# Rotary features gathered into two and a half projection tiles, and attention loads that gather the heads

## The chip, the cores and the metric

The kernel runs on one core of a Trainium2 chip. The metric is the device time of one execution in microseconds (us). The engines are named as in the profile: PE does matmuls (PEld is its weight load), DVE, ACT and POOL work on vectors, SP issues the DMAs. This kernel issues every DMA from SP.

## The reference, cut to what matters

One decoder layer runs over 1024 prompt tokens and 8 rows of 8 sampled tokens, 1088 tokens in all. One input projection feeds two groups: sliding-window attention with 16 query heads on 4 key/value heads (head dimension 64), and a Mamba-2 state-space group (SSD). Their outputs go through one output projection, and a SwiGLU feed-forward follows. Only the first 16 of a head's 64 features are rotated:

```python
q, k, v, z, xbc, dt_raw = jnp.split(h @ w_in, SPLIT_IDX, axis=-1)
q = rope_partial(q.reshape(b, L, ATT_HEADS, HEAD_DIM), pos)
k = rope_partial(k.reshape(b, L, ATT_KV_HEADS, HEAD_DIM), pos)

def rope_partial(x, pos):                 # ROT_DIM = HEAD_DIM // 4 = 16, half = 8
    xr = x[..., :ROT_DIM].astype(F32)
    x1, x2 = xr[..., :half], xr[..., half:]
    rot = jnp.concatenate([x1 * cos - x2 * sin, x2 * cos + x1 * sin], axis=-1)
    return jnp.concatenate([rot.astype(x.dtype), x[..., ROT_DIM:]], axis=-1)
```

Three results depend on the rotated keys beside the layer's output: the last 128 keys of the prompt are an output (`new_k_prompt`), and the sampled tokens' keys join the cached ones.

## The kernel before

**Tiling.** Activations lie feature-major: 128 features on the partitions, tokens along the row, in three chunks of 384, 384 and 320 tokens (`CH`). A weight tile is 1024 x 128: `load_w` (L118) brings it in two halves of 256 KB, ACT casts each to its high part (L123), POOL subtracts for the low part (L124). `gemm` (L133) multiplies in three passes (lines 140 to 142). One unit of the input projection (`in_unit`, L281) is one weight tile by one chunk: 24 matmuls into one of two PSUM buffers ("mm", the profile's `ip`), then an evacuation, which frees the buffer.

**Two evacuations.** `spill_evac` (L483) is one DVE multiply of PSUM by the row scale `Rx` into a staging tile (`stg`, L486), and a DMA to scratch in DRAM (L487). `rope_evac` (L678) is for rotated tiles: ACT copies PSUM to `ra` (L681), DVE shuffles partitions into `rb` (L683), POOL multiplies `rb` by the sine table (L684), DVE multiplies `ra` by the cosine table (L685) and adds both (L686), and a DMA goes to scratch (L687). The tables carry the row scale, and hold one and zero for features that do not rotate. Each head's 64 features stand together, so every q and k tile holds some rotated features: of the twelve tiles of `kvq` (L690), ten go through `rope_evac` (30 units) and two, the values, through `spill_evac` (6 units). `z_proj` follows with eight more spilled tiles.

**Order.** PE's order is written by hand: `weave(mixer, filler)` (L157) lets the mixer run, and the filler fill the time that the mixer grants. In the stage of this change the mixer is the SSD over its eight prompt chunks and the sampled tokens (`ssd`, with `ssd_a`, L515, and `ssd_b`, L573), and the filler is `kvq`, then `z_proj`, then the first output projection (L698 to L700). In the attention stage the filler goes on with `z_proj` and the output projection. The order on DVE, ACT, POOL and SP is set by a tile scheduler from the order of the code and from priorities; evacuations and weight loads are marked urgent. Once set, each engine runs strictly in its order.

**SSD names.** `d_0...` and `d_1...` are the two groups. `YI` are PSUM products of a chunk, evacuated into `y` on DVE (L584). For the sampled tokens, `xh` (ACT, L590) and `xw` (DVE, L591) are the split operand of the state products `H` (L635, L636); POOL scales the old state (`d_0h`, L638) and DVE adds `H` (L640).

**Attention.** `blk_a` (L725) handles one block of 128 tokens and one pair of key heads (16 in all): it loads q by one DMA (L730), k by two (L733) and v by one (L735), PE transposes v (`vt`, L737), ACT casts k (`KW`, L742), and ACT and POOL split q (`A`, L749 and L750). Its load buffers are double. `att_sample` (L837) loads the same things once for the sampled tokens, by six DMAs (L849 to L851). The last 128 keys go to their output by two DRAM-to-DRAM copies (`o_kp`, L811).

Of the kernel before, what the change touches and what calls it, by code (L numbers as in the profile page):

```python
# [23 lines left out]
HD = 64  # L24
NFF = 22
# [9 lines left out]
def hybrid_layer(ctx, tc, A):  # L35
# [26 lines left out]
    # split operands of a chunk in half tiles of four feature tiles each, in numbered slots  # L62
# [37 lines left out]
    class Extra:  # L100
        # weight slots cut out of a larger tile
# [31 lines left out]
    def gemm(out, ws, xs, step=3, only=None):  # L133
        # three passes of split operands; yields the time on the tensor engine
# [18 lines left out]
    def weave(mixer, filler):  # L153
        # the filler yields its time on the tensor engine, or None while its operands are not there;
        # the mixer yields how long the filler may hold the tensor engine before it goes on
        credit = 0.0
        for gap in mixer:  # L157
            credit += gap
            while credit > 0:
                try:  # L160
                    cost = next(filler)
                except StopIteration:
                    break
                if cost is None:
                    break
                credit -= cost
# [4 lines left out]
    def rsqrt_cols(st, nb, inv, name):  # L171
        # 1/sqrt(st * inv + eps), one token per partition: bit-level first guess, Newton to float32
# [14 lines left out]
    def rms(groups, n, inv, name, gap, keep=None):  # L187
        # groups of tiles; the sum over a group's tiles and partitions is the sum of squares of each token
# [32 lines left out]

    def finish(gen):
# [6 lines left out]
    # scratch in DRAM  # L229
    q_scr = [dr.tile([P, 4, TOK], F32, name="q_scr%d" % p) for p in range(2)]  # L230
    k_scr = [dr.tile([P, TOK], F32, name="k_scr%d" % p) for p in range(2)]
# [104 lines left out]
    with pool("conv") as cvp:  # L336
# [38 lines left out]
        with pool("norm") as tp:  # L375
# [15 lines left out]
            # the tensor engine's clock comes up while the first operands are on their way  # L391
# [11 lines left out]
            def dt_mm(c, k):  # L403
                # four feature tiles at a time, in four column groups of the array
# [19 lines left out]
            # the first chunk by feature tile, as they come in; its evacuation waits for the row scale  # L424
# [82 lines left out]
    with pool("ssd") as sd, pool("rope") as rp:  # L507
# [5 lines left out]
        def ssd_a(c, gi):  # L513
            # token-major x scaled by dt and by the tail decay; masked C.B; decay weights
# [154 lines left out]
        shuf = list(range(8, 16)) + list(range(8)) + list(range(16, 32))  # L669
# [8 lines left out]
        def rope_evac(dst):  # L678
            def f(c, c0, n, o):
                a = rp.tile([P, n], F32, tag="ra", bufs=2, name="ra")  # L680
                s.copy(a, o)  # L681
                b = rp.tile([P, n], F32, tag="rb", bufs=2, name="rb")
                v.stream_shuffle(b, a, shuf)  # L683
                g.tensor_mul(b, b, sinT[:, c0:c0 + n])  # L684
                v.tensor_mul(a, a, cosT[:, c0:c0 + n])  # L685
                v.tensor_add(a, a, b)  # L686
                dma(dst[:, c0:c0 + n], a)  # L687
            return f

        def kvq():  # L690
            for p in range(2):
                yield from in_proj(2 * p, rope_evac(k_scr[p]))
                yield from in_proj(2 * p + 1, spill_evac(v_scr[p]))
            for gi in range(4):
                for p in range(2):
                    yield from in_proj(4 + 4 * p + gi, rope_evac(q_scr[p][:, gi, :]))
            done.add("q")
# [27 lines left out]
    def blk_a(ap, n, p, KW, vts):  # L725
# [4 lines left out]
        dma(qb, q_scr[p][:, :, b0:b0 + P])  # L730
        kd = ap.tile([P, 2, P], F32, tag="kd", bufs=2, name=nm + "k")
        for hh in range(2):
            dma(kd[HD * hh:HD * hh + HD], k_scr[p][:, b0:b0 + P].rearrange("(e f) t -> f e t", e=2))  # L733
# [76 lines left out]
    for p in range(2):  # L810
        dma(A["o_kp"][p], k_scr[p][:, SEQ - P:SEQ])  # L811
# [24 lines left out]
    # sampled tokens: one batch row at a time, all heads on the rows  # L836
    def att_sample(ap):  # L837
# [9 lines left out]
        with tc.high_priority():  # L847
            for p in range(2):
                dma(qs[p], q_scr[p][:, :, SEQ:])  # L849
                dma(kvn[:, p, 0, :], k_scr[p][:, SEQ:])  # L850
# [77 lines left out]
    def gate(c, at=None):  # L928
        # y * silu(z), its norm, and the split of the result
# [131 lines left out]
    with pool("chain") as kp:  # L1061
        # the first FFN tiles go chunk by chunk
# [23 lines left out]
    with pool("ffn") as fp:  # L1086
        # the cache rows that only move up, in the time when little else is loaded
# [5 lines left out]
        for gi, G in enumerate(FFG):  # L1093
# [51 lines left out]
            else:  # L1145
                # the last feature tiles go chunk by chunk, with the last norm and the residual behind them
# [17 lines left out]
                for c, (c0, n) in enumerate(CH):  # L1164
# [13 lines left out]
                    # the second feature tile's operands come in behind the first one's products  # L1178
# [21 lines left out]
def _consts():  # L1200
# [16 lines left out]
    cos = np.ones((P, TOK), f)  # L1217
    sin = np.zeros((P, TOK), f)
    for e in range(2):
        o = e * HD  # L1220
        cos[o:o + 8] = co
        cos[o + 8:o + 16] = co
        sin[o:o + 8] = -si
        sin[o + 8:o + 16] = si
# [12 lines left out]
def _layout(x):  # L1237
# [10 lines left out]
    q = w[:, 0:1024].reshape(DM, 2, 2, 4, HD).transpose(0, 1, 3, 2, 4).reshape(DM, 1024)  # L1248
    k, v_, z = w[:, 1024:1280], w[:, 1280:1536], w[:, 1536:2560]
    xs, bcm, dt = w[:, 2560:3584], w[:, 3584:4096], w[:, 4096:4112]  # L1250
    d["w_in"] = blk(np.concatenate([k[:, :P], v_[:, :P], k[:, P:], v_[:, P:], q, bcm, xs, z], 1))
# [58 lines left out]
```

## Time and profile before

| what | value |
|---|---|
| median of 3 runs | 1768.01 us (1766.32 to 1768.69) |
| span of the profiled execution | 1755.4 us |
| PE busy in it | 1650.0 us, 94% |
| DVE, ACT, POOL busy | 931.4, 629.0, 659.3 us |

The profile is of one execution; its span runs from its first to its last recorded instruction. The 12.6 us between span and median lie outside what the trace records. The stage of this change is the stretch from 190 to 455 us (keys, values and queries beside the SSD), and the attention stage is 455 to 735 us.

### The profile page before, as it was taken

Reading aid. Unit: us, or ns where it says so; the run is one execution under the profiler, and the core shown is the slowest. Engines: PE = TensorE matmul, PEld = TensorE weight load, DVE = VectorE, ACT = ScalarE, POOL = GpSimd, SP = SyncE. Lnnn points to the kernel's source line nnn. Section 1 sums busy time; section 2 is a strip of 40 time slices with the busy share of each in tenths; the row PEclk is TensorE's granted clock in tenths of the full one; section 3 lists DMA queues with packets and bytes.
Section 4 is the critical chain, followed back from the end, with each engine's and each line's share of the span. In section 5 each row is a group of like instructions: output and inputs, shape, how many; then the busy total and the mean of one; then the engine's idle time right before and its main releaser. Section 6 shows DMA issues by size and latency. Waiting matters only on the chain. (4 is left out here: it accounts for less than half of the span.)

```text
span 1755.4 us, 26644 instructions
## 1 busy us (share of the span) xinstructions
PE 1650.0 (94%) x9959; PEld 1553.4 (88%) x9959; DVE 931.4 (53%) x1977; ACT 629.0 (36%) x1416; POOL 659.3 (38%) x537
## 2 busy tenths in 40 slices
PE   9899998888888998999988999999999999999995
PEld 6899987766776787898987999999999999999995
DVE  7796778886588898455877401221312212121347
ACT  5242344441376676554543332112121121211221
POOL 5262366666743333323655322222222221221432
PEclk9899999998999999999999999999999999999997
DMA  5022564444652351543554111111111111110233
GB/s 184 30 85 101 166 177 136 134 125 157 208 153 84 93 156 59 167 148 94 180 179 141 47 49 32 49 52 32 55 41 47 44 38 49 41 55 22 82 102 102
DMA packets 144945, 171.12 MB, mean 97 GB/s; under 512 B 16624, under 2 KB 105200, under 8 KB 144784
## 3 DMA queue, kind: packets, MB, share of 16 engines
q1 hardware_dynamic: 144816, 169.43, 31.6%
q8 instruction: 78, 1.28, 0.3%
q14 instruction: 51, 0.42, 0.1%
HBM read 135.33 MB, written 36.28 MB: 98 GB/s over the span
## 5 line engine op out<-in xcount | busy, mean ns | idle before, releaser
L1027 DVE TENSOR_TENSOR sg<-sg,ou 128x384 f32<-128x384 f32 (+1 forms) x66 | 35.0, 531 | 393.4 <-PE ou L142 392.7
L1138 DVE TENSOR_TENSOR YP<-YP,od 128x384 f32<-128x384 f32 (+1 forms) x168 | 89.0, 531 | 126.9 <-PE od L142 126.7
L124 POOL TENSOR_TENSOR wg_1l<-wg_1r,wg_1h 128x512 fp32r<-128x512 f32 x20 | 25.9, 1295 | 211.5 <-ACT wg_1h L123 211.5
L1028 ACT CAST ffh<-sg 128x384 fp32r<-128x384 f32 (+1 forms) x66 | 32.6, 495 | 188.9 <-DVE sg L1027 188.5
L124 POOL TENSOR_TENSOR wi_1l<-wi_1r,wi_1h 128x512 fp32r<-128x512 f32 x40 | 56.7, 1418 | 63.7 <-ACT wi_1h L123 60.2
L1023 ACT ACTIVATE sg<-og 128x384 f32<-128x384 f32 (+1 forms) x66 | 31.0, 471 | 131.9 <-PE og L142 125.2
L124 POOL TENSOR_TENSOR wi_0l<-wi_0r,wi_0h 128x512 fp32r<-128x512 f32 x40 | 58.3, 1458 | 30.6 <-ACT wi_0h L123 26.2
L1029 DVE TENSOR_TENSOR ffl<-sg,ffh 128x384 fp32r<-128x384 f32 (+1 forms) x66 | 42.8, 649 | 33.9 <-ACT ffh L1028 33.8
L140 PE MATMUL ip<-x1h,wi_0h 128*128 128x384 f32 x128 | 48.0, 375 | 11.8 <-ACT ra L681 5.2
L124 POOL TENSOR_TENSOR wos_1l<-wos_1r,wos_1h 128x512 fp32r<-128x512 f32 x24 | 33.1, 1377 | 65.3 <-ACT wos_1h L123 58.3
L124 POOL TENSOR_TENSOR woa_1l<-woa_1r,woa_1h 128x512 fp32r<-128x512 f32 x24 | 35.0, 1456 | 49.6 <-ACT woa_1h L123 38.4
L363 DVE SCALAR_TENSOR_TENSOR cacc<-cbuf,vec,cacc 128x1112 f32<-128x1112 f32 x36 | 52.3, 1455 | 0.7
L140 PE MATMUL ip<-x0h,wi_0h 128*128 128x384 f32 x128 | 47.4, 371 | 3.5 <-DVE cbuf L350 3.5
L124 POOL TENSOR_TENSOR wd_1l<-wd_1r,wd_1h 128x384 fp32r<-128x384 f32 (+1 forms) x7 | 6.8, 974 | 105.2 <-ACT wd_1h L123 105.2
L140 PE MATMUL ip<-x0h,wi_1h 128*128 128x384 f32 x128 | 45.6, 356 | 0.0
L142 PE MATMUL ip<-x0h,wi_0l 128*128 128x384 f32 x128 | 44.0, 344 | 1.5 <-POOL wi_0l L124 1.5
L140 PE MATMUL ip<-x1h,wi_1h 128*128 128x384 f32 x128 | 45.1, 353 | 0.0
L124 POOL TENSOR_TENSOR wg_0l<-wg_0r,wg_0h 128x512 fp32r<-128x512 f32 x21 | 27.4, 1304 | 45.6 <-ACT wg_0h L123 45.6
L142 PE MATMUL ip<-x1h,wi_0l 128*128 128x384 f32 x128 | 44.3, 346 | 0.0
L141 PE MATMUL ip<-x0l,wi_0h 128*128 128x384 f32 x128 | 43.8, 342 | 0.4 <-DVE x0l L261 0.4
L141 PE MATMUL ip<-x1l,wi_0h 128*128 128x384 f32 x128 | 44.2, 345 | 0.0
L684 POOL TENSOR_TENSOR rb<-rb,sinT 128x384 f32<-128x384 f32 (+1 forms) x30 | 36.0, 1198 | 21.2 <-DVE rb L683 17.5
(837 smaller groups left out, 6215.0 us busy)
## 6 DMA issues: line engine op xcount, KB each, us to landing
wi_0r<-in_w_in SPq DMA_DIRECT2D x40, 256.0 KB
wi_1r<-in_w_in SPq DMA_DIRECT2D x40, 256.0 KB
wos_0r<-in_w_os SPq DMA_DIRECT2D x24, 256.0 KB
wos_1r<-in_w_os SPq DMA_DIRECT2D x24, 256.0 KB
woa_0r<-in_w_oa SPq DMA_DIRECT2D x24, 256.0 KB
woa_1r<-in_w_oa SPq DMA_DIRECT2D x24, 256.0 KB
wg_0r<-in_w_g SPq DMA_DIRECT2D x22, 256.0 KB
wg_1r<-in_w_g SPq DMA_DIRECT2D x22, 256.0 KB
```

The costliest lines, as they stand in the source:

```text
L124: (eng or g).tensor_sub(lo, raw, fr(hi))
L140: t.matmul(out, lhsT=wh, rhs=xh, start=k == 0, stop=False)
L141: t.matmul(out, lhsT=wh, rhs=xl, start=False, stop=False)
L142: t.matmul(out, lhsT=wl, rhs=xh, start=False, stop=k == n - 1)
L363: v.scalar_tensor_tensor(acc[:, :L], buf[:, k:k + L], vec[:, cw + k:cw + k + 1], acc[:, :L], ALU.mult, ALU.add)
L684: g.tensor_mul(b, b, sinT[:, c0:c0 + n])
L1023: s.activation(sg, og[:, :n], AF.Silu)
L1027: v.tensor_mul(sg, sg, ou[:, :n])
L1028: s.copy(hi[:, c0:c0 + n], sg)
L1029: v.tensor_sub(lo[:, c0:c0 + n], sg, fr(hi[:, c0:c0 + n]))
L1138: v.tensor_add(YP[m][:, c0:c0 + n], YP[m][:, c0:c0 + n], o[:, :n])
```

## The change

The host permutes the columns of `w_in` for q and k so that the rotated features of all heads stand together. The twelve tiles become: tile 0, 64 rotated key features and 64 key features that do not rotate; tile 1, the other 128 of those; tiles 2 and 3, values; tiles 4 and 5, the rotated query features of either pair of key heads; tiles 6 to 11, all other query features. Tiles 4 and 5 go through `rope_evac` whole, tile 0 in its first 64 partitions, with one DVE multiply for the rest. That makes 9 units with rotation (three of them with the extra multiply) and 27 that are spilled. The scratch tensors `q_scr` and `k_scr` become `qr_scr`, `qn_scr`, `kr_scr` and `kn_scr`, and each load puts the heads together again: per attention block four DMAs for q and four for k instead of one and two, for the sampled tokens 16 instead of four beside the two of v, and four for `o_kp` instead of two.

```diff
+    def load_q(dst, p, t0, n):
+        for e in range(2):
+            for o, w, src in ((0, ROT, qr_scr[p]), (ROT, NRT, qn_scr[p])):
+                dma(dst[HD * e + o:HD * e + o + w],
+                    src[:, t0:t0 + n].rearrange("(g e r) t -> e r g t", g=4, e=2)[e])
+
+    def k_rows(p, t0, n):
+        for o, w, src in ((0, ROT, kr_scr), (ROT, NRT, kn_scr)):
+            yield o, w, src[2 * p * w:2 * p * w + 2 * w, t0:t0 + n].rearrange("(e r) t -> e r t", e=2)
...
-        def rope_evac(dst):
+        def rope_evac(dst, m=P, rest=None):
             def f(c, c0, n, o):
                 a = rp.tile([P, n], F32, tag="ra", bufs=2, name="ra")
-                s.copy(a, o)
+                s.copy(a[:m], o[:m])
                 b = rp.tile([P, n], F32, tag="rb", bufs=2, name="rb")
-                v.stream_shuffle(b, a, shuf)
-                g.tensor_mul(b, b, sinT[:, c0:c0 + n])
-                v.tensor_mul(a, a, cosT[:, c0:c0 + n])
-                v.tensor_add(a, a, b)
-                dma(dst[:, c0:c0 + n], a)
+                v.stream_shuffle(b[:m], a[:m], shuf)
+                g.tensor_mul(b[:m], b[:m], sinT[:m, c0:c0 + n])
+                v.tensor_mul(a[:m], a[:m], cosT[:m, c0:c0 + n])
+                v.tensor_add(a[:m], a[:m], b[:m])
+                dma(dst[:, c0:c0 + n], a[:m])
+                if rest is not None:
+                    x = stage(n, "stg")
+                    v.tensor_mul(x[m:], o[m:], Rx[c][m:])
+                    dma(rest[:, c0:c0 + n], x[m:])
             return f

         def kvq():
+            yield from in_proj(0, rope_evac(kr_scr, HD, kn_scr[0:HD]))
+            yield from in_proj(1, spill_evac(kn_scr[HD:]))
             for p in range(2):
-                yield from in_proj(2 * p, rope_evac(k_scr[p]))
-                yield from in_proj(2 * p + 1, spill_evac(v_scr[p]))
-            for gi in range(4):
-                for p in range(2):
-                    yield from in_proj(4 + 4 * p + gi, rope_evac(q_scr[p][:, gi, :]))
+                yield from in_proj(2 + p, spill_evac(v_scr[p]))
+            for p in range(2):
+                yield from in_proj(4 + p, rope_evac(qr_scr[p]))
+            for i in range(6):
+                yield from in_proj(6 + i, spill_evac(qn_scr[i // 3][P * (i % 3):P * (i % 3) + P]))
...
-        dma(qb, q_scr[p][:, :, b0:b0 + P])
+        load_q(qb, p, b0, P)
...
-            dma(kd[HD * hh:HD * hh + HD], k_scr[p][:, b0:b0 + P].rearrange("(e f) t -> f e t", e=2))
+            for o, w, src in k_rows(p, b0, P):
+                dma(kd[HD * hh + o:HD * hh + o + w], src.rearrange("e r t -> r e t"))
...
-        dma(A["o_kp"][p], k_scr[p][:, SEQ - P:SEQ])
+        for o, w, src in k_rows(p, SEQ - P, P):
+            dma(A["o_kp"][p].rearrange("(e f) t -> e f t", e=2)[:, o:o + w, :], src)
...
-                dma(qs[p], q_scr[p][:, :, SEQ:])
-                dma(kvn[:, p, 0, :], k_scr[p][:, SEQ:])
+                load_q(qs[p], p, SEQ, NS)
+                for o, w, src in k_rows(p, SEQ, NS):
+                    for e in range(2):
+                        dma(kvn[HD * e + o:HD * e + o + w, p, 0, :], src[e])
```

The cosine and sine tables now repeat over all partitions, and the shuffle pattern swaps eights in all 32 lanes. PE's order stays the same, matmul for matmul, but for the names of weights. What moves stands on the other engines.

**DVE, sampled tokens.** DVE's order around the sampled tokens' `d_0xw`, on which PE's state products wait. Before:

```order
L544 TENSOR_TENSOR d_1cb<-d_1bc,cst 64x64
L551 TENSOR_SCALAR d_1W<-d_1ac,ADT 64x64 x4
L584 SCALAR_TENSOR_TENSOR d_0y<-d_0xb,vec,d_0YI 128x64 x4
L683 STREAM_SHUFFLE rb<-ra 128x384
L685 TENSOR_TENSOR ra<-ra,cosT 128x384
L591 TENSOR_TENSOR d_0xw<-d_0xtl,d_0xh 64x512
L686 TENSOR_TENSOR ra<-ra,rb 128x384
```

and now:

```order
L561 TENSOR_TENSOR d_1cb<-d_1bc,cst 64x64
L568 TENSOR_SCALAR d_1W<-d_1ac,ADT 64x64 x4
L601 SCALAR_TENSOR_TENSOR d_0y<-d_0xb,vec,d_0YI 128x64 x2
L503 TENSOR_TENSOR stg<-ip,rs1Rk 128x384
L601 SCALAR_TENSOR_TENSOR d_0y<-d_0xb,vec,d_0YI 128x64 x2
L608 TENSOR_TENSOR d_0xw<-d_0xtl,d_0xh 64x512
```

The three rotary steps around `d_0xw` became one multiply from PSUM, inside the `d_0y` group. On POOL the row `rb<-rb,sinT` between `d_1W` and the weight subtraction `wi_1l` is gone; `wi_1l` and the four scalings of `d_0h` still follow.

**DVE, middle of the stage.** DVE's order at a change of SSD chunk in the stretch that is all queries. Before:

```order
L544 TENSOR_TENSOR d_1cb<-d_1bc,cst 128x128
L683 STREAM_SHUFFLE rb<-ra 128x384
L584 SCALAR_TENSOR_TENSOR d_0y<-d_0xb,vec,d_0YI 128x128
L685 TENSOR_TENSOR ra<-ra,cosT 128x384
L584 SCALAR_TENSOR_TENSOR d_0y<-d_0xb,vec,d_0YI 128x128
L686 TENSOR_TENSOR ra<-ra,rb 128x384
L584 SCALAR_TENSOR_TENSOR d_0y<-d_0xb,vec,d_0YI 128x128 x2
```

and now:

```order
L547 TENSOR_TENSOR d_1xdt<-d_1xT,ADT 128x512
L548 TENSOR_TENSOR d_1xtl<-d_1xT,ADT 128x512
L561 TENSOR_TENSOR d_1cb<-d_1bc,cst 128x128
L503 TENSOR_TENSOR stg<-ip,rs1Rk 128x384
L601 SCALAR_TENSOR_TENSOR d_0y<-d_0xb,vec,d_0YI 128x128 x4
```

The rotary steps that stood between the four `d_0y` rows are gone, and one multiply stands ahead of them.

**SP, start of the attention stage.** SP's order of DMA issues from the first query load to the first value load (`a_0q`, `a_0k` and `a_0vb` are a block's q, k and v; `wi` are halves of a `z` weight tile). Before:

```order
L730 DMA a_0q<-q_scr_78 128x4x128
L487 DMA z_scr<-stg 128x384
L120 DMA wi_0r<-in_w_in 128x512
L733 DMA a_0k<-k_scr_80 64x2x128 x2
L120 DMA wi_1r<-in_w_in 128x512
L735 DMA a_0vb<-v_scr_82 128x128
```

and now, from the fourth row on (ahead of it stand the first `qr_scr` load, a `z_scr` spill and a `wi_0r`):

```order
L228 DMA a_0q<-qn_scr_80 48x4x128
L122 DMA wi_1r<-in_w_in 128x512
L228 DMA a_0q<-qr_scr_78 16x4x128
L228 DMA a_0q<-qn_scr_80 48x4x128
L504 DMA z_scr<-stg 128x384
L122 DMA wi_0r<-in_w_in 128x512
L758 DMA a_0k<-kr_scr 16x2x128
L122 DMA wi_1r<-in_w_in 128x512
L758 DMA a_0k<-kn_scr 48x2x128
L758 DMA a_0k<-kr_scr 16x2x128
L758 DMA a_0k<-kn_scr 48x2x128
L760 DMA a_0vb<-v_scr_84 128x128
```

The value load is now the 15th issue from the first query load, where it was the seventh: eight loads of q and k stand ahead of it instead of three, two spills instead of one, and four weight halves instead of two.

## Rows read from the trace of the kernel before

**Rows 1.** Part 1 of the page: busy time, share of the span, instructions.

```profile
PE 1650.0 (94%) x9959; PEld 1553.4 (88%) x9959; DVE 931.4 (53%) x1977; ACT 629.0 (36%) x1416; POOL 659.3 (38%) x537
```

**Rows 2.** Stretches: bounds; us, PE, PEld, DVE, ACT, POOL busy (x); clock, DMA share, GB/s.

```profile
205.00:265.00 60.00, 59.19 (x416) 53.24 (x415) 47.07 (x99) 31.39 (x78) 35.46 (x24) 1.00 0.70 195
265.00:378.00 113.00, 98.00 (x674) 85.83 (x672) 93.89 (x187) 50.05 (x124) 75.10 (x54) 0.98 0.47 131
378.00:410.00 32.00, 21.89 (x97) 17.00 (x96) 23.39 (x37) 6.80 (x17) 16.88 (x14) 0.73 0.34 114
...
265.00:302.00 37.00, 32.92 (x223) 29.64 (x221) 30.24 (x61) 16.07 (x41) 24.33 (x18) 0.95 0.46 129
302.00:378.00 76.00, 65.09 (x453) 56.20 (x452) 63.64 (x127) 33.97 (x84) 50.77 (x37) 1.00 0.47 132
```

**Rows 3.** Waits of PE, 265 to 378 us: total us, times, longest.

```profile
PE ip L140 <- ACT ra L681: 5.2, 4, 1.8
PE d_0YI L580 <- DVE d_1y L584: 4.4, 4, 2.0
```

**Rows 4.** Waits of PE, 378 to 410 us.

```profile
PE d_0H L636 <- DVE d_0xw L591: 6.9, 1, 6.9
PE d_0YI L580 <- DVE d_1y L584: 1.6, 1, 1.6
```

**Rows 5.** Instructions on tile ra by stretch: length, DVE, ACT busy, clock, DMA.

```profile
205.00:265.00 60.00, 9.42 (x15) 1.83 (x4) 1.00 0.70 195
265.00:378.00 113.00, 42.15 (x57) 6.32 (x14) 0.98 0.47 131
```

**Rows 6.** Tiles ra and stg, 190 to 455 us: ns min/median/max, starts, forms.

```profile
L685 DVE TENSOR_TENSOR ra<-ra,cosT x30: 493/1110/2226, 194.5 to 445.0; 128x384 f32<-128x384 f32 x20, 128x320 f32<-128x320 f32 x10
...
L486 DVE TENSOR_TENSOR stg<-ip,rs0Rk x10: 547/554/558, 206.5 to 507.8; 128x384 f32<-128x384 f32 x10
```

**Rows 7.** Line L591 on DVE; POOL's timeline from 394 us (start, us).

```profile
L591 DVE TENSOR_TENSOR d_0xw<-d_0xtl,d_0xh x1: 6747/6747/6747, 394.5 to 394.5; 64x512 fp32r<-64x512 f32 x1
L591 DVE TENSOR_TENSOR d_1xw<-d_1xtl,d_1xh x1: 676/676/676, 430.4 to 430.4; 64x512 fp32r<-64x512 f32 x1
...
394.03 1.35 POOL L684 TENSOR_TENSOR rb<-rb,sinT 128x384 f32<-128x384 f32 x1
395.35 1.25 POOL L124 TENSOR_TENSOR wi_1l<-wi_1r,wi_1h 128x512 fp32r<-128x512 f32 x1
396.56 4.09 POOL L638 TENSOR_TENSOR d_0h<-d_0h,d_0en 128x512 f32<-128x512 f32 x4
```

**Rows 8.** SP's issues of attention loads: ns min/median/max, starts.

```profile
L730 SPq DMA_DIRECT2D a_0q<-q_scr x8: 549/557/614, 458.3 to 632.8; - x8
...
L733 SPq DMA_DIRECT2D a_1k<-k_scr x16: 574/590/1222, 467.4 to 649.5; - x16
```

**Rows 9.** Timeline of SP and PE as the attention starts.

```profile
458.31 0.61 SPq L730 DMA_DIRECT2D a_0q<-q_scr  x1
462.08 0.44 SPq L735 DMA_DIRECT2D a_0vb<-v_scr  x1
...
465.64 0.30 PE L737 MATMUL a_0vt<-cst,a_0vb 128*128 128x128 f32 x1 [1.38 <-DMA wi_1r<-in_w_in]
472.64 0.33 PE L737 MATMUL a_1vt<-cst,a_1vb 128*128 128x128 f32 x1 [2.25 <-DMA a_1vb<-v_scr]
```

**Rows 10.** Timeline of SP and ACT, a key load and its first use.

```profile
571.51 1.24 SPq L733 DMA_DIRECT2D a_0k<-k_scr  x2
...
598.08 0.41 ACT L742 CAST KW<-a_0k 128x256 fp32r<-128x256 f32 x1
```

**Rows 11.** Timeline of SP, ACT and PE behind the sampled tokens' loads.

```profile
732.88 1.59 SPq L120 DMA_DIRECT2D woa_0r<-in_w_oa  x1
...
740.99 0.62 ACT L123 CAST woa_0h<-woa_0r 128x512 fp32r<-128x512 f32 x1 [5.09 <-DMA woa_0r<-in_w_oa]
...
745.73 0.34 PE L140 MATMUL op<-o0h,woa_0h 128*128 128x384 f32 x1
```

More of the change, by code (lines that the diff above doesn't have):

```diff
@@ L24 @@
 HD = 64
+ROT = 16
+NRT = HD - ROT
 NFF = 22
@@ L227, in finish @@
             return e.value
-    q_scr = [dr.tile([P, 4, TOK], F32, name="q_scr%d" % p) for p in range(2)]
-    k_scr = [dr.tile([P, TOK], F32, name="k_scr%d" % p) for p in range(2)]
+    qr_scr = [dr.tile([P, TOK], F32, name="qr_scr%d" % p) for p in range(2)]
+    qn_scr = [dr.tile([3 * P, TOK], F32, name="qn_scr%d" % p) for p in range(2)]
+    kr_scr = dr.tile([4 * ROT, TOK], F32, name="kr_scr")
+    kn_scr = dr.tile([4 * NRT, TOK], F32, name="kn_scr")
     v_scr = [dr.tile([P, TOK], F32, name="v_scr%d" % p) for p in range(2)]
@@ L666, in ssd @@
             yield from ssd_b(prev)
-        shuf = list(range(8, 16)) + list(range(8)) + list(range(16, 32))
+        shuf = [16 * i + (j + 8) % 16 for i in range(2) for j in range(16)]
         cosT = rp.tile([P, TOK], F32, name="cosT")
@@ L1216, in _consts @@
     co, si = np.cos(ang), np.sin(ang)
[L1217 to L1224, printed above, removed]
+    cos = np.tile(co, (P // 8, 1))
+    sin = np.tile(np.concatenate([-si, si], 0), (P // ROT, 1))
     scanm = np.ones((16, TOK), f)
@@ L1246, in blk, with flat @@
         return m.reshape(kk // P, P, mm // P, P).transpose(2, 1, 0, 3)
-    q = w[:, 0:1024].reshape(DM, 2, 2, 4, HD).transpose(0, 1, 3, 2, 4).reshape(DM, 1024)
-    k, v_, z = w[:, 1024:1280], w[:, 1280:1536], w[:, 1536:2560]
+    q = w[:, 0:1024].reshape(DM, 2, 2, 4, HD).transpose(0, 1, 3, 2, 4)
+    k, v_, z = w[:, 1024:1280].reshape(DM, 4, HD), w[:, 1280:1536], w[:, 1536:2560]
+    def flat(m):
+        return m.reshape(DM, -1)
     xs, bcm, dt = w[:, 2560:3584], w[:, 3584:4096], w[:, 4096:4112]
-    d["w_in"] = blk(np.concatenate([k[:, :P], v_[:, :P], k[:, P:], v_[:, P:], q, bcm, xs, z], 1))
+    d["w_in"] = blk(np.concatenate([flat(k[..., :ROT]), flat(k[..., ROT:]), v_, flat(q[..., :ROT]),
+                                    flat(q[..., ROT:]), bcm, xs, z], 1))
     d["w_dt"] = np.pad(dt.reshape(8, P, 16).transpose(1, 0, 2), ((0, 0), (0, 0), (0, 16)))
```

## The prediction, made before the changed kernel was run

> **What bounds the kernel now.** I read the page's busy times first: PE is busy 94% of the span, no other engine over 53% [rows 1]. PE's matmuls and their order are untouched, so the change can gain only what PE loses in gaps, plus matmul time lost to a low clock. Next I cut the stage into stretches [rows 2]. From 205 to 265 us, with half of the units rotated, PE idles 60.00 - 59.19 = 0.8 us. From 265 to 378 us, where every filler unit is a rotated query tile, it idles 113.00 - 98.00 = 15.0 us. From 378 to 410 us, around the first sampled-token group, it idles 32.00 - 21.89 = 10.1 us, with a mean clock of 0.73. What differs between the first two is rotary work: on tile `ra` alone DVE spends 42.15 us of 113 in the second, 9.42 of 60 in the first [rows 5]; in the second it stands still for 113.00 - 93.89 = 19 us even so [rows 2], so order counts as well as load. PE's own waits say the same: in the middle stretch it waits for the PSUM buffer that ACT's rotary copy frees (5.2 us) and for SSD products that DVE evacuates late (4.4 us for `d_1y`) [rows 3]; in the next, once for 6.9 us for `d_0xw` on DVE, and 1.6 us for `d_1y` [rows 4].
>
> **Middle stretch: forecast -10, bounds 0 to -15.** Of 30 rotated units 9 remain, so 21 lose three DVE operations, an ACT copy and a POOL multiply, and get one DVE multiply (three more serve the mixed tile, so 24 multiplies are added). Where they remain matters: tiles 4 and 5, rotated whole, are the first query tiles, six units that stand where the first six of the 57 / 3 = 19 rotated units of this stretch stood [rows 5]. That is its first third, 265 to 302 us, whose idle time, 37.00 - 32.92 = 4.1 us [rows 2], I leave as it is. In the other 76 us some 13 units lose their rotation. A rotated unit's DVE work is 3 x 42.15 / 57 = 2.2 us [rows 5], the multiply instead 0.55 [rows 6]: 13 x 1.65 = 21 us less, so DVE there falls from 63.64 us [rows 2] to about 43, a busy share of 0.56, below the 0.78 (47.07 of 60) of the stretch that PE crosses almost without idling [rows 2], and the ACT and POOL steps leave the chain that frees PSUM. These 76 us hold 76.00 - 65.09 = 10.9 us of idle time [rows 2], of which I leave 0.8 x 76 / 60 = 1.0: -9.9, taken as -10. Upper end: all 15.0 us, if relief behind the first third reaches into it. Lower end: nothing, if the gaps come from strictly ordered queues, whatever stands in them.
>
> **Sampled tokens: forecast -12, bounds 0 to -18.** `d_0xw` took 6747 ns, its twin `d_1xw` 676 for the same shape [rows 7]. It started at 394.5 and ended at 401.2, while POOL ran six instructions without a gap, 394.03 to 400.65. The first of the six is a rotary multiply, and it is gone. Then POOL goes from `d_1W` to the weight subtraction `wi_1l`, which must wait for ACT's cast of that tile; in the gap `d_0xw` can run. In the order it stands ahead, but DVE now has one more PSUM multiply and half of `d_0y` before it, so that it may still meet the scalings of `d_0h`. I put the gap at some 2 in 3 and take the wait as gone: -6.9 and -1.6 of the `d_1y` wait [rows 4]. The low clock goes with it. A mean of 0.73 between the levels 1.0 and 0.5 (2.4 and 1.2 GHz) means 54% of 32 us, or 17 us, at the low one; if the 8.5 us of those waits lie in it, some 8.5 us of matmuls ran at half speed and would take 4.3 less. Sum -12.8; I take -12 and leave some for a shorter wait. Upper end: all idle time, 10.1, and all the clock's loss with it, 17 x 0.5 = 8.5, makes -18. Lower end: `d_0xw` is held again, 0.
>
> What the row shows is an instruction held through six POOL instructions [rows 7]. The Trainium skill ("SBUF — State Buffer", section "Who interferes with whom") says that a VectorE instruction with two SBUF inputs is blocked by a GpSimd instruction that reads SBUF until that one is done, and that one with at most one SBUF input is not. By the rule alone the hold would end with the instruction in progress, the gap would not be needed, and the -12 would be sure; the sum would be the same, and rival 1 less likely. The trace speaks against a hold of one instruction; it agrees on the second half: the spill multiply, one input from PSUM, never left 547 to 558 ns, where the two-input multiply spread from 493 to 2226 [rows 6].
>
> Gains together: -22.
>
> **Loads at the attention's start: forecast +5, bounds 0 to +10.** Issues of the old loads take 0.56 and 0.59 us [rows 8]; I take 0.6 for each new one, since these two differ by 0.03 us where one moves four times the other's bytes. Before, the first value load was issued 462.08 - 458.31 = 3.8 us after the first query load, and PE's transpose of it started at 465.64, so just 3.6 us later, after a wait [rows 9]. Now it is the 15th issue: five more gathers, one more spill and two more weight halves. 14 x 0.6 = 8.4 us, 4.6 more. One of the halves needs a raw buffer that POOL frees behind its first split of `a_0q`, whose loads come later too: about 1 us. PE waited 1.4 us there already, so no slack hides it: 4.6 to 5.6 us. The second block's transpose waited 2.2 us at 472.64 and gets five more issues, 3 us, inside the same delay. I take +5. Upper end: the two delays add, 5.6 + 3, and some clock. Lower end: PE is late enough with the `z` tiles that stand before the transpose.
>
> **The other loads of the attention: +1, bounds 0 to +5.** Each of the other 14 blocks has five issues more, 2.9 us of SP. In the steady part a key load is issued at 571.51 and first used at 598.08 [rows 10]: 26.6 us ahead, which hides 2.9. Some early blocks have less.
>
> **Sampled tokens' loads: +3.5, bounds 0 to +6.** There are 12 issues more (18 for 6), 12 x 0.6 = 7.2 us, ahead of the weight `woa_0r`. Issued at 732.88, its cast started at 740.99, and PE used it at 745.73 [rows 11]. From the cast's end (0.62 us) and a POOL subtraction of 1.25 (as in [rows 7]) to that use are 745.73 - 740.99 - 0.62 - 1.25 = 2.9 us of slack, and a little more, since the low part is used in the third pass only; I take 3.7. 7.2 - 3.7 = 3.5. Upper end: a shortage of weights goes on over the next tiles; lower end: buffers ahead of it absorb it.
>
> **Key output and other spills: +0.5, bounds 0 to +2.** `o_kp` makes two more issues, nothing waits for them but their place on SP; the mixed tile's second part adds three stores, in a stretch where PE idles 0.8 us. Column order, tables and host work cost nothing on the chip.
>
> Costs together +10, net -12. The profiled span is 1755.4 us; the 12.6 us between it and the median lie outside it and are carried over. 1768.0 - 12 = **1756.0 us**.
>
> **Rivals.** (1) *`d_0xw` is held again.* DVE comes to it late and meets the four scalings of `d_0h`; of the -12 only -1 is left. -10 - 1 + 10 = -1: 1767.0 us. For it: the hold outlasted the one rotary multiply by five instructions [rows 7]. Against it: the gap before `wi_1l`. Chance 0.22. (2) *Slower: the gathers are dear to issue.* The dearest issue of a key load took 1222 ns against a median of 590 [rows 8]. If each gather of 16 or 48 partitions takes that, 32 gathers that nothing hides (8 in each of the first two blocks, 16 for the sampled tokens) cost 32 x 0.64 = 20.5 us more; with the net -12 that is +8.5: 1776.5 us. It makes the kernel slower from 12 / 32 = 0.38 us more a gather on, 0.97 us each. For it: a gather's source is cut into two or four groups of rows. Against it: a query load of 128x4x128 and a key load of 64x2x128 differ by 0.03 us. Chance 0.08. (3) *All comes back.* Both stretches lose nearly all idle time and the low clock, -14 and -16 of the bounds, and all the loads together cost 2, because PE reaches the attention with its `z` weights still to come: -28, 1740.0 us. For it: ACT and POOL lose work too, and both feed every unit's weights. Chance 0.15. That the change doesn't do what it says would need rotary steps left behind the first third; the order has none there.
>
> The Trainium skill ("DMA: Bandwidth & Descriptors", section "Rules for kernel authors") speaks against this change: small transfers should be coalesced, since those under 64 KB are mostly overhead, and two halves of the partitions should be one transfer. By it rival 2's sum, 1776.5 us, would be the time, if the overhead lay in the issue. No row of before shows a load of 16 partitions.
>
> **How the numbers follow.** The forecast's band, 1747 to 1763, has 0.50; rival 1 0.22, rival 2 0.08, rival 3 0.15, anything else 0.05. A measurement of this kernel can tell about 0.2%, 3.5 us, from no change. Faster by more: the band (0.50), rival 3 (0.15) and a part of rival 1 (0.05): 0.70. Within 0.2%: the middle of rival 1: 0.12. Slower by more: the rest of rival 1 (0.05), rival 2 (0.08) and the other (0.05): 0.18. The range of 8 in 10 goes from 1740, rival 3's time, to 1770, just over rival 1's; outside lie half of rival 3, the upper tail of rival 1, and rival 2.
>
> **What would show it.** Right: over the last two thirds of the queries PE's idle time falls to about 1 us, no wait for ACT's `ra` remains there, `d_0xw` takes under 1.5 us; the first value transpose waits about 5 us, gather issues have a median near 0.6 us, and a wait for `woa` shows near 745 us. Wrong: `d_0xw` of 6 us again (rival 1), waits of PE for spill multiplies or `y` of over 5 us there (the lower end of -10), gather issues of 1 us and more (rival 2), or waits for loads throughout the attention.

## The result and the profile after

The changed kernel takes 1747.32 us in the median of 4 runs (1742.97 to 1751.08), the kernel before 1768.35 on the same chip: a ratio of 0.9895, 95% interval 0.9876 to 0.9915, so 15 to 22 us less. On another chip it was 1748.79 against 1763.54, ratio 0.992 (0.989 to 0.9951). The forecast was 1756.0 in a range of 1740 to 1770.

The page's busy times of the changed kernel, which answer to [rows 1]:

```profile
PE 1655.3 (95%) x9959; PEld 1560.4 (89%) x9959; DVE 881.5 (50%) x1917; ACT 624.0 (36%) x1397; POOL 631.4 (36%) x516
```

DVE loses 50 us and POOL 28, and PE runs the same 9959 matmuls. Next the stretches of the stage in the changed kernel, cut at the same matmuls of PE's order as the table further down (columns as in [rows 2]):

```profile
221.40:280.00 58.60, 57.64 (x416) 51.77 (x413) 37.58 (x90) 28.36 (x71) 34.76 (x24) 1.00 0.59 170
280.00:315.60 35.60, 31.59 (x212) 28.44 (x211) 27.88 (x56) 14.40 (x35) 23.59 (x18) 0.95 0.49 143
315.60:368.60 53.00, 53.00 (x383) 47.41 (x383) 40.78 (x90) 26.51 (x66) 34.97 (x24) 1.00 0.57 169
368.60:394.10 25.50, 25.50 (x155) 19.42 (x152) 12.22 (x28) 5.73 (x14) 12.65 (x11) 1.00 0.52 171
441.50:459.00 17.50, 11.55 (x62) 11.15 (x61) 4.61 (x22) 7.63 (x21) 9.09 (x8) 0.80 0.52 143
```

The third and fourth lines are the gain: behind the six rotated query units, and around the sampled tokens, PE no longer idles, and the clock, 0.73 in [rows 2], is 1.00. The second line, the six rotated units, still holds 4.0 us of idle time. The last is the attention's start, with 6 us.

The longest wait of PE that is left in each of three places of the changed kernel: as the SSD starts (205 to 222 us), at the attention's start (441 to 460) and behind the sampled tokens' loads (676 to 745); us in total, times, longest:

```profile
PE d_1xT L543 <- DVE d_0xtl L548: 2.8, 1, 2.8
...
PE a_0vt L762 <- DMA a_1q<-qr_scr: 6.0, 1, 6.0
...
PE op L144 <- DVE woa_0l L126: 4.0, 1, 4.0
```

In the second line the view names a query load as what ended the wait, which it infers from semaphores. What PE transposes there is the first block's values, `a_0vb`; SP issued that load at 448.80 us, and the transpose started at 450.93.

And the operation that [rows 7] showed at 6747 ns:

```profile
L608 DVE TENSOR_TENSOR d_0xw<-d_0xtl,d_0xh x1: 1374/1374/1374, 380.6 to 380.6; 64x512 fp32r<-64x512 f32 x1
```

One correction to the reading of before. In a run whose own time is known, the span lies 1.8 us under it (1749.3 for 1751.08). So the first trace of before, with its span of 1755.4, was of an execution of about 1757, and not of 1768 with 12.6 us outside. The kernel was therefore traced again on the chip of the changed kernel's second trace.

### The profile page after: what moved, and what is told of

Read it like the earlier page. It is cut to its first block, busy times and chain, and to the rows that moved or that the text cites. A ratio compares the mean times of both kernels' runs of the same rounds, so it can differ in the third digit from the quotient of the medians.

```text
span 1749.3 us, 26692 instructions
## 1 busy us (share of the span) xinstructions
PE 1655.3 (95%) x9959; PEld 1560.4 (89%) x9959; DVE 881.5 (50%) x1917; ACT 624.0 (36%) x1397; POOL 631.4 (36%) x516
## 5 line engine op out<-in xcount | busy, mean ns | idle before, releaser
L1057 DVE TENSOR_TENSOR ffl<-sg,ffh 128x384 fp32r<-128x384 f32 (+1 forms) x66 | 42.8, 650 | 33.9 <-ACT ffh L1056 33.8
L126 POOL TENSOR_TENSOR woa_1l<-woa_1r,woa_1h 128x512 fp32r<-128x512 f32 x24 | 33.7, 1405 | 64.8 <-ACT woa_1h L125 57.9
L144 PE MATMUL ip<-x0h,wi_1l 128*128 128x384 f32 x128 | 43.8, 342 | 0.0
```

Source lines behind the costliest of these rows:

```text
L126: (eng or g).tensor_sub(lo, raw, fr(hi))
L144: t.matmul(out, lhsT=wl, rhs=xh, start=False, stop=k == n - 1)
L1057: v.tensor_sub(lo[:, c0:c0 + n], sg, fr(hi[:, c0:c0 + n]))
```

## The experiments

PE's order is the same in all kernels, so the n-th matmul is the same work in each, and a stretch of PE can be compared from matmul to matmul. This table gives the length of each stretch in us, from the start times of these matmuls in the traces (the kernels are told of below):

| stretch (matmuls) | before, first | before again | changed again | loads only | evac. only | no rotation | merged, loads first |
|---|---|---|---|---|---|---|---|
| convolution and SSD start (700-1150) | 74.2 | 74.1 | 79.1 | 74.9 | 78.0 | 78.9 | 79.5 |
| values, keys (1150-1560) | 58.2 | 58.8 | 58.6 | 64.8 | 57.4 | 59.8 | 58.6 |
| first third of the queries (1560-1770) | 37.1 | 37.0 | 35.7 | 30.3 | 34.7 | 29.6 | 35.3 |
| other queries (1770-2150) | 63.7 | 63.2 | 52.9 | 63.5 | 54.2 | 52.9 | 53.1 |
| sampled tokens' state (2150-2300) | 40.5 | 40.9 | 26.3 | 40.8 | 25.2 | 25.5 | 25.4 |
| attention's start (2560-2620) | 14.4 | 13.2 | 17.1 | 19.0 | 12.1 | 18.3 | 14.5 |
| early attention (2620-3000) | 78.7 | 77.9 | 73.6 | 74.8 | 81.7 | 75.5 | 74.4 |
| late attention (3600-3800) | 39.4 | 40.3 | 42.8 | 42.9 | 38.5 | 43.0 | 44.6 |
| behind the sampled loads (3800-4150) | 61.4 | 61.4 | 67.0 | 64.4 | 61.4 | 67.8 | 61.9 |
| sampled attention (4150-4400) | 40.3 | 47.4 | 41.9 | 38.9 | 43.3 | 42.0 | 43.7 |

Left out are the start (0-700), in which all kernels do the same work and which took 137.1 to 138.8 us with the old evacuations and 135.3 to 141.2 with the new, two stretches in which all agree within 2 us, and the 950 us from matmul 4400 on, alike within 7. A stretch by itself says less than it seems to: loads only, with the rotation of before, takes 6.0 us more than before again for the values and keys and 6.7 less in the first third of the queries, 95.1 against 95.8 us together. Idle time moves between these two neighbours, so they are best read as one.

**Both kernels again.**

> The kernel before itself, for a trace of an execution whose own time is known. Theory A (the trace of before that the prediction was read from is of an execution at the fast edge): the span is 1.8 us under the run's own time, as it was in the changed kernel (1749.3 for 1751.1), so about 1764 to 1768 us, and the 10 us more than the first trace's 1755.4 lie in the stretch of the queries and the sampled tokens. Rival B (some 12 us of a run lie outside the trace): a span of 1755 again beside a time of 1768.

> The changed kernel itself, for a second trace. Theory A: again 1743 to 1751 us, with the sampled tokens' d_0xw at about 1.4 us and the first value transpose of the attention waiting 6 us; the 5 us that PE fell behind between 190 and 215 us in the first trace are this kernel's and come again. Rival B: they belong to one execution and are gone.

Measured: before 1764.44 us (1760.11 to 1771.13, 10 runs), profiled span 1762.8; the changed kernel 1748.79, span 1747.4. The wait of 2.8 us at the SSD's start, the 6 us at the first value transpose and `d_0xw` at 1.36 us came again, so theory A holds, but for one thing. The second trace of before is 7.4 us longer than the first, and that lies not where theory A put it but in one stretch behind the attention. Its line in the first trace (columns as in [rows 2]):

```profile
753.30:793.60 40.30, 39.22 (x252) 36.59 (x250) 17.96 (x54) 22.89 (x50) 10.11 (x7) 1.00 0.39 118
```

and in the second:

```profile
752.20:799.50 47.30, 46.46 (x252) 43.03 (x249) 18.05 (x54) 22.89 (x50) 10.05 (x7) 0.82 0.31 100
```

The same 252 matmuls, the same other engines, one wait of 1.1 and 0.8 us in them: but the clock is 1.00 in one and 0.82 in the other.

**The two halves of the change apart.** Loads only, in the kernel before:

```diff
-        dma(qb, q_scr[p][:, :, b0:b0 + P])
+        for e in range(2):
+            for o, w in ((0, 16), (16, 48)):
+                dma(qb[HD*e+o:HD*e+o+w], q_scr[p][HD*e+o:HD*e+o+w, :, b0:b0+P])   # k, o_kp, sampled tokens alike
```

> The kernel before with the new number of loads alone: each q and k load is cut into the pieces of 16 and 48 partitions that the change has, out of the old scratch; rotation as before. Theory A (the loads cost what the prediction put, +10, and in the aligned traces +11): 1768 + 10 = 1778 us, with a wait of 5 to 6 us at the first value transpose and one of 4 us or so for the output weights behind the sampled tokens' loads. Rival B (in the kernel before PE is late enough that they are hidden): within 3 us of before.

Measured: 1767.61 us, ratio 1.004 (1.0019 to 1.0062), so 3 to 11 us more: between the two theories, some 7 us by the ratio. Evacuations only, in the changed kernel; it leaves out putting the heads together again:

```diff
-            yield from in_proj(0, rope_evac(kr_scr, HD, kn_scr[0:HD]))
+            yield from in_proj(0, rope_evac(k_scr[0][0:HD], HD, k_scr[0][HD:]))   # q alike
-        load_q(qb, p, b0, P)
+        dma(qb, q_scr[p][:, :, b0:b0 + P])                                       # all loads as before
```

> The change with the new evacuations alone: columns permuted and nine rotated units as in the change, but scratch and loads in the old shapes, so that the heads' features are not put together again and attention reads them in another order. Theory A (gains and costs add): the changed kernel less the loads' 10 us, 1747 - 10 = 1737 us. Rival B (part of the gain exists only because the loads have nothing to hide behind): 1744 us or more.

Measured: 1739.22 us, ratio 0.9877 (0.9839 to 0.9915), so 15 to 28 us less. The two halves add up within the noise: by the ratios +7 and -22 make -15, and the whole made -14 on that chip; by the medians +4 and -24 make -20, against -15. The table adds something. The loads make the attention's start 4 to 6 us longer, but the early attention behind it is 3 to 8 us shorter in the kernels with gathers than in those without. Waits of PE in the early attention, of before again (472.8 to 550.7 us):

```profile
PE ip L140 <- DVE stg L486: 3.6, 1, 3.6
PE a_1o L800 <- DVE a_1PT L113: 2.6, 2, 1.3
PE a_1s L768 <- DVE a_1mx L774: 2.6, 2, 1.7
```

and of the changed kernel again (459.1 to 532.8):

```profile
PE a_1s L793 <- DVE a_1mx L799: 3.1, 3, 1.3
PE a_1o L825 <- DVE a_1PT L115: 2.9, 2, 1.5
...
PE ip L142 <- DVE stg L503: 1.0, 1, 1.0
```

The wait of 3.6 us for a spilled `z` tile is in the kernel before and, as long, in the one with the evacuations only; in the changed kernel, loads only and no rotation it is 1.0 or not there. So what the start costs is mostly made up for within 75 us. That the stall at the start is what shortens the early attention is not shown. Between before again and changed again PE's idle time there falls by 2.4 us only (12.2 to 9.8), and the rest is the clock (0.96 and 0.98). And the last kernel of this section (merged, loads first), which stalls less at the start, has this wait too and still takes 74.4 us (452.8 to 527.3 us in it):

```profile
PE ip L142 <- DVE stg L497: 2.9, 1, 2.9
```

Behind the sampled tokens' loads nothing is made up for: 61.4 with the old loads, 64.4 to 67.8 with the change's gathers.

**What held `d_0xw`.** In the kernel before, one word:

```diff
-            v.tensor_sub(xtw, xf, fr(xth[:NS]))
+            g.tensor_sub(xtw, xf, fr(xth[:NS]))
```

> The kernel before with one word changed: the sampled tokens' xw subtraction runs on POOL instead of DVE, in POOL's order ahead of wi_1l and of the scalings of the state. Theory A (PE's 6.9 us wait was DVE's xw being held while POOL ran without a gap, and the low clock came of the wait): xw takes 1.3 us there, PE waits under 2 us for it, and the span falls by 8 to 11 us. Rival B (the wait is that of late work on DVE as a whole): PE waits about as long, now for POOL or for the d_0y work, and the time stays within 3 us of before.

Measured: 1761.26 us, ratio 0.9976 (0.9946 to 1.0006), which is not clear of no change. PE's wait fell from 6.9 to 2.3 us and the stretch from 40.9 to 36.8; the clock there went from 0.75 to 0.81 only:

```profile
PE d_0H L636 <- POOL d_0xw L591: 2.3, 1, 2.3
PE d_0YI L580 <- DVE d_1y L584: 1.6, 1, 1.6
PE ip L140 <- ACT ra L681: 1.3, 1, 1.3
```

The wait came down nearly as theory A said; the price isn't its 8 to 11 us. Of the 14.6 us that the change gains here, `d_0xw` on POOL gives 4.1, with 2.3 us of its wait left. In the other 10.5 the other rotary waits are gone too, and the clock is 1.00; no run takes these away with `d_0xw` still held, so how they share the 10.5 is not shown. And the reason for the hold was tried in the changed kernel:

```diff
             g.tensor_mul(W, W, cb.unsqueeze(1).broadcast_to([nt, 8, nt]))
+            if smp and gi == 1:
+                with tc.high_priority():
+                    hb = rp.tile([P, 384], F32, tag="rb", bufs=2, name="rb")
+                    Wf = W.rearrange("p h t -> p (h t)")[:, :384]
+                    g.tensor_mul(hb[:NS], Wf, Wf)
```

> The changed kernel with one more POOL instruction, a multiply of 64 x 384 that nothing uses, right behind POOL's d_1W of the sampled tokens, where the rotary multiply stood. It takes some 0.9 us and closes the gap of 0.45 us in which DVE's d_0xw went through (1.37 us long in the changed kernel). Theory A (a DVE instruction with two inputs in SBUF waits until POOL has a gap): d_0xw is held until the scalings of the state are through, takes 6 us or more, PE waits 5 us or more for it and its clock falls; the stretch is 8 to 12 us longer, the time some 1757 us. Rival B (it waits only for the POOL instruction in progress): d_0xw takes 1 to 2.5 us, and the time grows by 1 us at most.

Measured: 1748.96 us, ratio 0.9924 (0.9898 to 0.995), the changed kernel's within its interval. The timelines of POOL and DVE in this kernel (start, us):

```profile
375.88 1.29 POOL L572 TENSOR_TENSOR d_1W<-d_1W,d_1cb 64x512 f32<-64x512 f32 x1 [5.96 <-DVE stg L503]
377.24 1.15 POOL L577 TENSOR_TENSOR rb<-d_1W 64x384 f32<-64x384 f32 x1
378.36 1.27 POOL L126 TENSOR_TENSOR wi_1l<-wi_1r,wi_1h 128x512 fp32r<-128x512 f32 x1
379.60 4.10 POOL L660 TENSOR_TENSOR d_0h<-d_0h,d_0en 128x512 f32<-128x512 f32 x4
...
376.34 1.37 DVE L613 TENSOR_TENSOR d_0xw<-d_0xtl,d_0xh 64x512 fp32r<-64x512 f32 x1
```

The gap ahead of `wi_1l` is filled, and `d_0xw` takes 1.37 us all the same: it waits for `d_1W` to end at 377.17 and goes through. Theory A's reason, that a long gap is needed, falls. A short one remained: the added instruction reads `d_1W` and so starts 0.07 us behind its end, where POOL's rows of before follow each other without any. That such a gap isn't needed either is shown by other instructions in the trace of before, here a cosine multiply with two inputs in SBUF beside POOL's row:

```profile
223.91 2.21 DVE L685 TENSOR_TENSOR ra<-ra,cosT 128x384 f32<-128x384 f32 x1
...
223.33 2.38 POOL L555 TENSOR_TENSOR d_0W<-d_0W,d_0cb 128x1024 f32<-128x1024 f32 x1 [1.32 <-DVE d_0cb L544]
225.67 1.33 POOL L684 TENSOR_TENSOR rb<-rb,sinT 128x384 f32<-128x384 f32 x1
```

It ends at 226.12, 0.4 us behind `d_0W`, and POOL's next instruction followed without a gap. In that trace 102 `TENSOR_TENSOR` operations of DVE took over 0.3 us longer than the shortest of their line and shape and saw a POOL instruction end; 101 were through before a second one ended, 41 of these with POOL's next following without a gap, and the other is `d_0xw`. That is the Trainium skill's rule ("SBUF — State Buffer", section "Who interferes with whom"): blocked until the instruction in progress is done. The 6.75 us of `d_0xw`, in three traces with the rotary pair ahead of it (before twice, loads only), stand against it; in the ten traces without that pair and with `d_0xw` on DVE it took 1.36 to 1.37. Nor is it quite alone: in both traces of the changed kernel (199.98 to 202.13 us in the second) and in five others a cosine multiply was held through one whole `wi_1l` after the instruction in progress. So a DVE instruction mostly goes through at the next change of POOL's instructions, but can lose that turn; what decides it, and why `d_0xw` lost five running, is open.

**What the nine rotated units still cost.** The changed kernel with the rotation left out:

```diff
-                s.copy(a[:m], o[:m])
...
-                v.tensor_add(a[:m], a[:m], b[:m])
-                dma(dst[:, c0:c0 + n], a[:m])
+                x = stage(n, "stg")
+                v.tensor_mul(x, o, Rx[c])
+                dma(dst[:, c0:c0 + n], x[:m])
```

> The changed kernel with the rotation left out: the nine rotated units get the one multiply of all others, so q and k are not rotated; loads as in the change. It shows what the nine units still cost. Theory A (the first units of the SSD lose 5 us to the mixed tile, the six rotated query units 4 us and more): 8 to 12 us less than the changed kernel, some 1738 us; d_0ac's first load is issued 4 us earlier against PE's work. Rival B (rotated units cost PE nothing once few are left): within 3 us of the changed kernel.

Measured: 1740.59 us, ratio 0.9878 (0.9856 to 0.9899). The six rotated query units cost what theory A said: the first third of the queries takes 29.6 us instead of 35.7, with no idle time, and together with the stretch ahead of it 89.4 instead of 94.3. The mixed tile does not: the SSD's start is 78.9 us even without its rotation. The other trial on it turned the order of the first tiles:

```diff
-            yield from in_proj(0, rope_evac(kr_scr, HD, kn_scr[0:HD]))
-            yield from in_proj(1, spill_evac(kn_scr[HD:]))
             for p in range(2):
                 yield from in_proj(2 + p, spill_evac(v_scr[p]))
+            yield from in_proj(1, spill_evac(kn_scr[HD:]))
+            yield from in_proj(0, rope_evac(kr_scr, HD, kn_scr[0:HD]))
```

> The changed kernel with the order of its first four tiles turned: values first, then the 128 key features that don't rotate, the mixed tile last. Theory A (the first 5 us that the changed kernel loses to the kernel before, 205 to 215 us, are the mixed tile's three stores and late rotary steps, behind which SP holds the SSD's first d_0ac load): the loss is gone, d_0ac is issued 4 us or more earlier against PE's work, and the time falls by 4 to 5 us to some 1743 us. Rival B (the loss is contention on the DMA queue, or sits wherever the first units are): within 2 us of the changed kernel.

Measured: 1750.41 us, ratio 0.9911 (0.9886 to 0.9936), no better than the changed kernel. The SSD's start fell from 79.1 to 77.1 us, but the first third of the queries, now with the mixed tile's three units just ahead of it, rose from 35.7 to 39.8. The windows of the SSD's start show what the 5 us are made of, in before again:

```profile
205.00:212.20 7.20, 6.43 (x46) 5.71 (x46) 6.05 (x13) 5.39 (x14) 2.46 (x1) 1.00 0.89 261
```

and in the changed kernel again:

```profile
208.90:221.10 12.20, 8.93 (x46) 8.04 (x46) 7.36 (x16) 8.04 (x21) 3.84 (x2) 0.72 0.76 221
```

46 matmuls each: 2.5 us more of idle time, and 2.5 more of matmul time at a clock of 0.72. The wait is for DVE's first scaled `x`, which stands behind the SSD's first `d_0ac` load; without rotation a wait of 2.3 us for `d_0cb` takes its place. Which moved row on DVE, ACT or SP begins it is not settled.

**Cheaper gathers.** First, part of them issued by ACT:

```diff
+        ld = s.dma_start if n == 0 else dma
-                dma(kd[HD * hh + o:HD * hh + o + w], src.rearrange("e r t -> r e t"))
+                ld(kd[HD * hh + o:HD * hh + o + w], src.rearrange("e r t -> r e t"))     # v alike
-                load_q(qs[p], p, SEQ, NS)
+                load_q(qs[p], p, SEQ, NS, s.dma_start)                                   # k alike
```

> The changed kernel with part of its gathers issued by ACT instead of SP: k and v of the first block of both key pairs, and q and k of the sampled tokens. Theory A (what they cost is SP's row of issues: 6 us at the first value transpose, 5 to 6 us at the output weights behind the sampled tokens): both waits shrink by half or more, and the time falls by 5 to 8 us to some 1741 us. Rival B (the gathers' transfers, not their issues, are late, or ACT now holds casts back in their place): within 2 us of the changed kernel, or slower.

> The two edits above together on the changed kernel. Theory A (both losses are there and add): 1748 less 4.5 less 6, some 1737 us, which is the time of the kernel with the new evacuations and the old loads. Rival B: no better than the better one of the two alone.

Measured: 1748.48 us, ratio 0.9899 (0.9867 to 0.9931), and together with the turned order of the first tiles 1755.61, ratio 0.9937 (0.9909 to 0.9964). The attention's start did shrink, from 17.1 to 11.0 us, but the early attention grew from 73.6 to 83.2 and the stretch behind the sampled loads from 67.0 to 69.5. Waits of PE with ACT's gathers (478 to 520 and 700 to 745 us):

```profile
PE a_0s L794 <- ACT KW L768: 5.0, 1, 5.0
...
PE op L142 <- ACT woa_0h L125: 5.4, 1, 5.4
```

and ACT's own waits there (690 to 745 us):

```profile
ACT mix L1012 <- DMA kvn<-kr_scr: 7.6, 1, 7.6
ACT woa_0h L125 <- DMA kvn<-kr_scr: 5.0, 1, 5.0
```

On ACT the gathers stand ahead of casts that PE needs: rival B. So their number was cut instead. With one scratch tensor for both key pairs, one DMA brings two pairs' rows, and the buffers hold a block of both:

```diff
-        load_q(qb, p, b0, P)
+        if p == 0:                                   # qb, kd, vb hold both pairs, one buffer each
+            load_q(qb, b0, P)                        # 16x8x128 and 48x8x128 instead of 16x4x128, 48x4x128
```

> The changed kernel with scratch laid out so that one DMA serves both key pairs: 9 loads for a block's two pairs instead of 18, 9 for the sampled tokens instead of 18, in buffers of double size that are no longer doubled. Theory A (the loads' price is the row of issues): the wait for the output weights behind the sampled tokens' loads goes nearly away, 4 to 6 us less there; the start stays as it is (15 issues to the first value load); the time some 1743 us. Rival B (the loads' latency, now with one buffer, or what stands behind them takes its place): within 2 us of the changed kernel, or slower with waits for k and q through the attention.

```diff
+            with (tc.high_priority(offset=1500) if n == 0 else ExitStack()):
```

> The kernel above, with the loads of the first block ahead of the two weight tiles on SP: 11 issues to the first value load instead of 15, and no wait of SP for POOL among them. Theory A: the wait of 6 us at the first value transpose falls to 3 us or less, and the time is another 3 to 4 us lower, some 1740 us. Rival B (the weights that now come later hold PE up instead): no lower than the kernel above.

Measured: 1746.0 us, ratio 0.9899 (0.9874 to 0.9924), and with the first loads ahead 1739.32 us, ratio 0.9874 (0.9846 to 0.9901), the lowest ratio of all kernels that compute the whole layer. The stretch behind the sampled loads is back at 61.9 us, and with the first loads ahead the attention's start takes 14.5 us instead of the 19.7 of the merged kernel, and nothing behind it takes that back. Against the changed kernel's ratio (0.9895 and 0.992 on two chips) the intervals still overlap; the stretches are what shows the gain. The first value transpose in the last kernel:

```profile
PE a_0vt L763 <- issue: 3.2, 1, 3.2
```

## Why the prediction was right, and where it was not

The sum was -12, and the traces of one chip give -15.3 (the last matmul starts at 1750.7 and 1735.4). Of these, +3.8 at the start of the kernel and -5.5 in the sampled attention are not the change's: the start spreads as widely among kernels that do the same there, and the sampled attention is the stretch that differed between the two traces of before. The change's own stretches make -13.5. On the first chip the medians differ by 21.0 us; this pair of traces does not tell where the rest of that lies. The sum came out nearer than its terms: the gains were 26.2 us instead of 22 and the costs 12.7 instead of 10, and among the costs 5.0 us at the SSD's start, which no term had, stand in the place of the 5 us that the attention's start did not keep. That these two cancel is luck. Term by term:

- **Other queries, -10:** right. The stretch went from 63.2 to 52.9 us, and PE's idle time in it to zero. Leaving the first third out was right as well: it gained 1.3 of 37.0 us, and the run without rotation shows that six units there still cost some 5 (89.4 us instead of 94.3 with the stretch ahead). Which of the steps that went, DVE's three, ACT's copy or POOL's multiply, had held PE up is told apart by no run.
- **Sampled tokens, -12:** right in direction and near in size, -14.6: 10 us of idle time, and 4.7 in which the same matmuls ran at the higher clock (30.46 to 25.75 us of PE's time). The reason given for `d_0xw` failed: it needs no long gap, and taken off DVE by itself it gave 4.1. Rival 1 rested on that reason; without the rotary pair `d_0xw` took 1.36 to 1.37 us in all ten traces.
- **Attention's start, +5:** the wait is there, 6.0 us, and the stretch 3.9 us longer, as worked out. What failed is that it would stay: 4.3 us come back in the early attention, 2.4 of them idle time, in which the wait for a spilled tile goes from 3.6 to 1.0 us. The prediction priced the stall without asking what the same loads would do to the waits behind it; that the stall itself uses up the later wait is not shown, and the merged kernel with the first loads ahead speaks against it (14.5 and 74.4 us).
- **Other loads of the attention, +1:** 2.5 us in the late attention (40.3 to 42.8).
- **Sampled tokens' loads, +3.5:** 5.6 us (61.4 to 67.0), with the wait for `woa` that was named. The issues were cheaper than the 0.6 us that was taken: the loads' row on SP takes 8.7 us (712.00 to 720.72) instead of 3.4 (728.28 to 731.72), 5.3 more where 7.2 were put. What was too large is the term's other half, the slack of 3.7 us. With the loads alone it was there: 6.6 us more of issues (734.27 to 744.29 for the row) cost 3.0. In the changed kernel it was not. The prediction took the subtraction of this weight half for one of POOL, 1.25 us, right behind the cast. It is DVE's; in before it takes 0.69 us, from 741.64 on, right behind the cast. In the changed kernel's second trace it comes behind DVE's splits of the operand, 1.7 us after the cast's end, and takes 1.75:

```profile
729.60 0.62 ACT L125 CAST woa_0h<-woa_0r 128x512 fp32r<-128x512 f32 x1 [0.50 <-DMA woa_0r<-in_w_oa]
...
729.27 2.69 DVE L999 TENSOR_TENSOR o1l<-of,o1h 128x768 fp32r<-128x768 f32 x3
731.88 1.75 DVE L126 TENSOR_TENSOR woa_0l<-woa_0r,woa_0h 128x512 fp32r<-128x512 f32 x1
```

- **Key output and other spills, +0.5:** this is the step that missed a cost. The mixed tile and its stores were dismissed because PE hardly idled there before; the SSD's start next to it lost 5.0 us, also with rotation left out.
- **The 12.6 us outside the span:** wrong, it is 1.8. The trace of before was of a faster execution than the median. It did little harm, since the clock and not the stage's waits made the difference.

Rival 2, gathers that are dear to issue, is out. The changed kernel's query gathers (columns as in [rows 8]):

```profile
L228 SPq DMA_DIRECT2D a_0q<-qr_scr x16: 303/430/537, 438.6 to 629.3; - x16
L228 SPq DMA_DIRECT2D a_0q<-qn_scr x16: 303/424/1931, 440.0 to 629.8; - x16
```

A gather's issue is 0.42 to 0.43 us, less than the 0.56 of the whole load. The Trainium skill's advice to coalesce small transfers ("DMA: Bandwidth & Descriptors", section "Rules for kernel authors") is borne out all the same by the merged kernel, which gains 5.1 us behind the sampled loads with half the DMAs; what it saves here is SP's row of issues (4.4 us, 706.98 to 711.38, in the kernel with the first loads ahead). Rival 3, all comes back, put the gains at -30 and the costs at 2; they were -26 (1.3, 10.3 and 14.6) and 13 (5.0, 3.9 - 4.3, 2.5 and 5.6).

## What to carry to other kernels

Where one engine is the bound and its order is fixed, compare two kernels from matmul to matmul: it shows at once which stretch gained, which lost, and which loss is paid back later. A change that takes work off the chain of a buffer gains what the bound engine waited, and the clock that it lost by waiting; shortening one of several waits in a row, from 6.9 to 2.3 us, gained here 4.1 of 14.6 us. Loads that are cut into pieces cost their row of issues where nothing hides it; merging them across heads, and putting the first ones ahead of prefetched weights, brought that back.

## What had not been expected of the hardware

The same program was 1753.5 to 1772.7 us over 19 runs of one chip. In the two traces of before, the clock's level alone made 7 us in one stretch of 252 matmuls: a mean of 1.00 against 0.82 (the levels 2.4 and 1.2 GHz) behind waits of 1.1 and 0.8 us. In the changed kernel's second trace the mean there was 0.92 while PE was busy for the whole 42.0 us; why the level fell is not shown. And one DVE instruction was held for 6.75 us, with the same figure in three traces, where nearly all others that were held went on after the POOL instruction in progress.
